# Adds moved from GpSimd to VectorE, probability scaling from VectorE to ScalarE, and later stores, in a two-layer hybrid decoder on one Trainium2 core

## Chip and metric

The kernel runs on one core of one Trainium2 chip. The metric is the device time of one execution in microseconds (us); of several runs the median is taken. Engines are named as the profile names them: PE is TensorE (matrix products), PEld its weight loads, DVE is VectorE, ACT is ScalarE, POOL is GpSimd, and SP is SyncE, which here only issues DMA transfers. Every engine runs its instructions in order.

## What is computed

Two layers over a sequence of 512 positions with model width 2048. Each layer projects x with one wide matrix, runs three groups of attention heads of width 128, gates them, projects back, and normalises. Cut from the reference:

```
h = einsum('bsd,dn->bsn', x, w_in)       # fq fk fv fg | dq dk dv dg | iq ik iw | mq mg
y_fox = fox_attention(fq, fk, fv, cum_logf) * silu(fg)      # 6 heads, causal, forget bias
y_dsa = dsa_attention(rope(dq), rope(dk), dv, index) * silu(dg)   # 6 heads, top 128 keys
kv = einsum('bmd,dn->bmn', mem, w_mem_kv)                   # 256 memory tokens
y_mem = memory_attention(mq, k_mem, v_mem) * silu(mg)       # 4 heads
y = einsum('bsn,nd->bsd', concatenate([y_fox, y_dsa, y_mem]), w_out)
x = layer_norm(ALPHA * x + y, ln_gain, ln_bias)
```

All is float32. In each attention the probabilities are exp(score - max) divided by their row sum.

## The kernel before

**Precision.** A float32 operand is split in two: ACT copies it to a rounded "hi" (`split_hi`), DVE subtracts to get the rest "lo" (`split_lo`). Each product is three matmuls: hi by hi, hi by lo, lo by hi. So each weight half of 128 x 1024 that arrives as tile `raw` becomes `whi` and `wlo` before PE can use it.

**Stages of a layer**, in this order of weight chunks; a chunk has two halves:

- memory: `mv` (4 chunks, memory's values, two halves each) and `mk` (4 chunks, memory's keys). The results are split and stored to DRAM, as `vm` and `km`, and read again when the memory heads run. In layer 1 these chunks also carry, between them, the transposes of the first layer's normalised output (`next_x`).
- small and `iq`: the indexer.
- values (`vs`): twelve blocks of 512 columns of the input projection in six pairs, by a Strassen-like scheme with seven products to a pair: P1, P7, P2, Q6, Q4 (the first part, ten chunks a pair) and Q5, Q3 (the second part). P7's weight is T3, the sum of two blocks of the weight matrix, and Q5's is T1, also a sum. For pair 0 the sum is read from DRAM; for pairs 1 to 5 one block is loaded into `raw` and the other into tiles `other` (two of 512 columns to a half), and `pair_w` adds them, two adds of 128 x 512 for each half. During the first part DVE also selects the indexer's top keys (`top_keys`), one step a chunk, and in layer 1 scales residual rows (`residual_rows`).
- heads: 8 chunks (`c`) of the last query and key projections, between whose products the attention heads run: scores (`s`), Exp, scaling by the reciprocal sums, transposes of the probabilities (`pt`), product with the values (`po`). Rotated heads (d) go through `rope_parts`: two products with cosine and sine tables, then their sum.
- out: the output projection, again seven products to a pair, while the last heads end.

**What sets the order.** The program is written out in Python in one order, and each engine takes its own instructions in that order. Loads are issued by SP two chunks ahead (`load_w(i + 2)`), splits are written three halves ahead (`split_w(n + 3)`), pair adds four (`pair_w(n + 4)`); in each half the pair adds stand ahead of the split. Seven `raw` buffers and four each of `whi` and `wlo` limit how far the loads and the splits really run ahead. Small jobs beside the stream (stores, top keys, residual rows) are generators in a list: `begin(gen, wait)` starts one after `wait` ticks, and `tick` steps all of them; there are two ticks to a chunk, one after the first half and one at its end. Values' accumulating loads (`grow_w`, for Q6 from P7's buffer) are issued by POOL.

The heads are placed by a planner: `Clock` charges each instruction an assumed time on its engine (for ACT 0.00086 us per element and 0.08, plus 0.1 where the scale is a column; for DVE's `tensor_scalar` 0.0007 per element and 0.07), each step of a head names the engine that it needs and the earliest time, and `advance`, called between PE's products, writes the steps that fit. `ahead` adds 0.15 us behind ACT, 0.12 behind DVE and 0.3 behind POOL before the next step may follow. The planned times decide only the order; the real engines wait by semaphores.

**The lines that the change touches.** `pair_w` takes POOL for P7 and DVE for Q5. `rope_parts` adds on POOL. `attend` scales the probabilities with four `nc.vector.tensor_scalar` of 512, 256, 128 and 384 columns, 1280 in all, with the column `rec` as factor; its inner `turn` lets PE's transposes follow at DVE's time. `keep_values` starts the stores of `vm` after 1 tick, and the stores of `km` also start after 1; both are issued by SP.

Of the kernel before, what the change touches and what calls it, by code (L numbers as in the profile page):

```python
# [14 lines left out]
AF = mybir.ActivationFunctionType  # L15
ALU = mybir.AluOpType
# [9 lines left out]
H_FOX, H_DSA, H_MEM = 6, 6, 4  # L26
# [217 lines left out]
def kernel(  # L244
# [13 lines left out]
    clock = Clock()  # L258
    nc = Engines(tc.nc, clock)
# [11 lines left out]
    def uid(name):  # L271
        count[0] += 1
        return f"{name}_{count[0]}"
# [3 lines left out]
    def slot(name, dt=F32, w=512):  # L277
        t = slots.tile([P, w], dt, tag="s", name=uid(name))
        if name in COUNTED:
            out_now.append(t)  # L280
        return t
# [20 lines left out]
    def split_hi(src, hi):  # L302
        nc.scalar.activation(hi, src, AF.Copy)
# [13 lines left out]
    chunks = stream()  # L317
# [16 lines left out]
    def half(src, h):  # L334
        return src[:, h * H:(h + 1) * H]

    def load_w(i, pieces=2, some=(0, 1)):
        if i < len(chunks) and chunks[i][4][0] != "grown":
            kind, key = chunks[i][4]
            src = {"wall": lambda: wall[key], "sum": lambda: sums[key],  # L340
                   "pair": lambda: wall[key[0]]}[kind]()
            if chunks[i][0] == "out" and chunks[i][2][0] == "Q6":
                for h in some:
                    t = [slot("grown") for _ in range(2)]
                    raw.setdefault(i, []).append(t)
                    for c in range(2):
                        nc.sync.dma_start(t[c], half(src, h)[:, c * 512:(c + 1) * 512])
                return
            w = DM // pieces
            for c in range(pieces):  # L350
                if c * 2 // pieces not in some:
                    continue
                if c * 2 % pieces == 0:
                    raw.setdefault(i, []).append(raws.tile([P, H], F32, tag="raw", name=uid("raw")))
                nc.sync.dma_start(raw[i][-1][:, c * w % H:c * w % H + w], src[:, c * w:(c + 1) * w])
                if i < 3 and c * 2 % pieces == 0:
                    load_mem(2 * i + c * 2 // pieces)
                if kind == "pair":
                    for e in (2 * c, 2 * c + 1):
                        t = slot("other")  # L360
                        nc.sync.dma_start(t, wall[key[1]][:, e * 512:(e + 1) * 512])
                        others[i, e] = t

    others = {}

    def pair_w(n):

        i, h = divmod(n, 2)
        if i < len(chunks) and chunks[i][4][0] == "pair":
            for e in range(2):  # L370
                d = raw[i][h][:, e * 512:(e + 1) * 512]
                eng = nc.gpsimd if chunks[i][2][0] == "P7" else nc.vector
                eng.tensor_tensor(d, d, others.pop((i, 2 * h + e)), op=ALU.add)

    def grow_w(n):

# [79 lines left out]
    def load_mem(j):  # L456
        mem_raw[j] = slot("memraw")
        nc.sync.dma_start(mem_raw[j], memt_in[:, j * 512:(j + 1) * 512])
# [122 lines left out]
    km_d = [[dram.tile([P, 512], F32, name=f"km{l}{j}") for j in range(H_MEM)] for l in range(DEPTH)]  # L581
# [6 lines left out]
    def begin(gen, wait=0, last=False, whole=False, but=None):  # L588


        active.append([wait, gen, last, whole, but])
# [20 lines left out]
    ahead = {"PE": 0.2, "ACT": 0.15, "DVE": 0.12, "POOL": 0.3}  # L612
# [25 lines left out]
    def free(n, eng):  # L638
        banks["held"] -= n
        freed.extend([clock.at[eng] + 0.1] * n)  # L640
# [65 lines left out]
    def keep(*moves):  # L706
        for to, t in moves:
            nc.sync.dma_start(to, t.bitcast(F32))
        yield 1

    def keep_values(l, m, part, t):
        c = slice((2 * m + part) * HD, (2 * m + part + 1) * HD)
        begin(keep((vm_d[l].rearrange("h p c -> p h c")[:, :, c],
                    t.rearrange("p (h c) -> p h c", h=H_MEM))), 1)

    def mem_head(l, j):
        there = load_head(("mq", j), MEMQ, j)
# [63 lines left out]
    def rope_parts(ps, to, key):  # L781

        t1, t2 = slot("rope"), slot("rope")
        nc.vector.tensor_tensor(t1, ps, cos_d, op=ALU.mult)
        for a, b, n in HALVES:
            nc.vector.tensor_tensor(t2[a:a + n], ps[b:b + n], sin_d[b:b + n], op=ALU.mult)
        free(1, "DVE")
        yield "POOL",
        nc.gpsimd.tensor_tensor(t1, t1, t2, op=ALU.add)
        yield "ACT",  # L790
        hi, lo = slot("qh", F32R), slot("ql", F32R)
        split_hi(t1, hi)
        yield "DVE",
        split_lo(t1, hi, lo)
        to[key] = (hi, lo)
# [162 lines left out]
    def attend(l, turn_no, kind, h):  # L958
# [17 lines left out]
        else:  # L976
            assert l in chosen
            bt, pr = masks[l], {}
        q, k = qs.pop(key), ks.pop(key)
        del qk_at[key]  # L980
        nm, sums, rec = small("nm", 4), small("sums", 4), small("rec", 4)
# [31 lines left out]
        yield "DVE", 0, 0.0, after(scored, 3)  # L1013
        del q, k
        nc.vector.reciprocal(rec, sums)
        for qb in (3, 1, 0, 2):
            b, off, w = PACK[qb]
            c = slice(off, off + w)
            nc.vector.tensor_scalar(pr[b][:, c], pr[b][:, c], rec[:, qb:qb + 1], None, op0=ALU.mult)
        pt = {}  # L1020

        def turn(tb, kts):
            yield "PE", 1, clock.at["DVE"] + ahead["DVE"]
            tp = bank("pt")
            for kt in kts:
                _, toff = PT_PACK[kt]
                for qb in range(kt, 4):
                    b, off, w = PACK[qb]
                    nc.tensor.transpose(tp[:, toff + (qb - kt) * P:toff + (qb - kt + 1) * P],
                                        pr[b][:, off + kt * P:off + (kt + 1) * P], ident)  # L1030
            yield "ACT",
            w = PT_W[tb]
            both = raws.tile([P, H], F32R, tag="raw", name=uid("pthl")) if w == 512 else slot("pthl", F32R)
            pt[tb] = both[:, :w], both[:, w:2 * w]
            split_hi(tp[:, :w], pt[tb][0])
            yield "DVE",
            split_lo(tp[:, :w], *pt[tb])
            free(1, "DVE")
            turns.append(clock.at["DVE"] + ahead["DVE"])
# [462 lines left out]
    for i, (kind, l, j, col, _) in enumerate(chunks):  # L1502
# [30 lines left out]
        for h in range(2):  # L1533
# [28 lines left out]
            if kind == "out" and late:  # L1562
# [6 lines left out]
                if len(kept) == 16:  # L1569
# [3 lines left out]
                    for c in (0, 256):  # L1573
                        ps = bank("z")
                        c = slice(c, c + 256)
# [19 lines left out]
            elif kind == "mv":  # L1595
                for m in range(2):
                    for nn in range(2):
                        k = 4 * col + 2 * h + nn
                        c = (k % 2) * 256 + m * P
# [3 lines left out]
            elif kind == "mk":  # L1603
                for kk in range(8):
                    k = 8 * h + kk
                    m = memT[k // 2]
                    c = (k % 2) * 256
# [16 lines left out]
        if kind == "mk":  # L1624
            t = slot("kmem", F32R)
            split(ps[:, :256], t[:, 0:256], t[:, 256:512])
            begin(keep((km_d[l][j], t)), 1)
            del t
            if j == 3:
                load_index_tables()  # L1630
        elif kind == "mv" and col == 3:
            for m in range(2):
                hi, lo = slot("vh", F32R), slot("vl", F32R)
                split(out_ps[m], hi, lo)
                for part, t in enumerate((hi, lo)):
                    keep_values(l, m, part, t)
                del hi, lo, t
        elif (kind, j) in HEAD_CHUNKS:
            flow(chunk_parts((kind[0], j), kind[1], ps))
        elif kind == "vs":  # L1640
            if col == 1:
                val_out(name, pair, zs)
                if name in VAL_ENDS:
                    del chains[VAL_CHAIN[name], pair], zs
        elif kind == "small":
            sm = slot("sm")
            nc.scalar.activation(sm, ps, AF.Copy)
            r = slice(96, 96 + H_FOX)
            nc.scalar.activation(sm[r], ps[r], AF.Identity, bias=bfc[r, l:l + 1])
            t = index_rope(ps, 64, 0, nc.vector)  # L1650
            kh2, kl2 = slot("kh2", F32R), slot("kl2", F32R)
            for r in (0, 64):
                nc.scalar.activation(kh2[r:r + 64], t[:64], AF.Copy)
                nc.vector.tensor_tensor(kl2[r:r + 64], t[:64], kh2.bitcast(F32)[:64],
                                        op=ALU.subtract)
            idx["k"] = (kh2, kl2)
            begin(small_work(l, sm))
            del sm, t
        elif kind == "iq":
            t = index_rope(ps, P, P, nc.gpsimd)  # L1660

            begin(index_parts(j, t), 1)
            del t
            if j == 0:
                begin(index_scores(l), 3, last=True, whole=True)
                begin(first_operands(), last=True)
            if j == 7:
                begin(val_operands(), 3, last=True)
            if j == 7:
                index_tabs.clear()  # L1670
# [126 lines left out]
```

## Time and profile before

| | |
|---|---|
| median of 3 runs | 1906.19 us (1903.26 to 1906.65) |
| profiled execution | 1903.6 us, span 1901.8 us |
| granted TensorE clock | 0.998 |
| busy in the span | PE 1876.5 us, DVE 1601.2, ACT 1003.7, POOL 555.7 |
| DMA | 491.01 MB, mean 258 GB/s |

The span is from the first to the last instruction of the profiled execution. In rows of groups, "x80 | 118.2, 1538 | 67.8 <-..." means 80 instructions, 118.2 us busy, 1538 ns each on average, and 67.8 us for which the engine was idle just before them, with what ended that. Rows of the timeline begin with the start in us from the span's start and the duration; square brackets hold the idle time before. All instructions carry line L228, a helper, so they are told apart by their tiles: `v` values, `c` chunks of other projections, `z` output, `pt` transposed probabilities, `bt` and `pr` the probabilities of the two kinds of heads. L355 is the issue of weight loads, L361 that of `other`, L708 the stores of `vm` and `km`. Rows of windows give start, end and length, then busy us and instructions of PE, PEld, DVE, ACT and POOL, the granted clock, the DMA engines' share and GB/s.

### The profile page before, as it was taken

What the parts mean: (1) busy time and instruction counts of PE and PEld (TensorE: products, weight loads), DVE (VectorE), ACT (ScalarE), POOL (GpSimd) and SP (SyncE); (2) the same over time, 40 slices, a digit from 0 to 9 for tenths busy, and PEclk for the clock granted to TensorE, in tenths of its full rate; (3) what the DMA queues carried; (4) which work ended last, traced back from release to release, by engine and by line L of the source; (5) the groups of instructions that cost most, each with busy time, mean ns of one, the idle gap of its engine ahead of it and who ended that gap; (6) DMA issues with size and microseconds to landing.
All of it is one profiled execution on the core that took longest, in us unless ns stands there. A gap on an engine that the chain in (4) does not pass through costs nothing. (4 is left out here: it accounts for less than half of the span.)

```text
span 1901.8 us, 27038 instructions
## 1 busy us (share of the span) xinstructions
PE 1876.5 (99%) x9218; PEld 1596.8 (84%) x9218; DVE 1601.2 (84%) x2519; ACT 1003.7 (53%) x1546; POOL 555.7 (29%) x699
## 2 busy tenths in 40 slices
PE   9999999999999999999999999999999999999997
PEld 8998888888888888888889987788888888888886
DVE  6889788988776888988877898999997768889888
ACT  5676444445455555555476754443454555555552
POOL 0131443333113333230041223443231133342401
PEclk9999999999999999999999999999999999999999
DMA  9886988879999788696578869999799997886965
GB/s 348 288 249 165 288 256 260 286 235 292 337 349 292 190 250 209 212 239 232 176 241 288 263 175 278 293 297 308 238 302 344 342 291 201 262 195 207 305 205 140
DMA packets 198007, 491.01 MB, mean 258 GB/s; under 512 B 19296, under 2 KB 72544, under 8 KB 193004
## 3 DMA queue, kind: packets, MB, share of 16 engines
q1 hardware_dynamic: 158028, 324.60, 49.9%
q0 software_dynamic: 39840, 164.68, 35.2%
q8 instruction: 72, 1.18, 0.2%
q14 instruction: 67, 0.55, 0.1%
HBM read 435.70 MB, written 122.71 MB: 294 GB/s over the span
## 5 line engine op out<-in xcount | busy, mean ns | idle before, releaser
L228 DVE TENSOR_TENSOR wlo<-raw,whi 128x1024 fp32r<-128x1024 f32 (+1 forms) x513 | 671.3, 1317 | 185.6 <-ACT whi L228 181.3
L228 ACT ACTIVATE whi<-raw 128x1024 fp32r<-128x1024 f32 (+1 forms) x513 | 538.8, 1056 | 506.3 <-PE v L228 248.7
L228 PE MATMUL v<-wlo,vxh 128*128 128x512 f32 x768 | 300.0, 391 | 3.6 <-DVE wlo L228 3.6
L228 PE MATMUL v<-whi,vxh 128*128 128x512 f32 x768 | 300.6, 391 | 0.0
L228 PE MATMUL v<-whi,vxl 128*128 128x512 f32 x768 | 299.2, 390 | 0.0
L228 PE MATMUL v<-whi,xh 128*128 128x512 f32 x576 | 224.2, 389 | 0.0
L228 PE MATMUL v<-whi,xl 128*128 128x512 f32 x576 | 224.1, 389 | 0.0
L228 PE MATMUL v<-wlo,xh 128*128 128x512 f32 x576 | 224.1, 389 | 0.0
L228 POOL DMA_DIRECT2D v<-vraw x144 | 94.6, 662 | 419.4 <-ACT vraw L228 230.7
L228 PE MATMUL c<-xh,whi 128*128 128x512 f32 (+1 forms) x544 | 203.7, 374 | 0.0
L228 PE MATMUL c<-xh,wlo 128*128 128x512 f32 (+1 forms) x544 | 198.6, 365 | 0.0
L228 PE MATMUL c<-xl,whi 128*128 128x512 f32 (+1 forms) x544 | 198.1, 364 | 0.0
L228 PEld LDWEIGHTS v<-wlo,vxh 128*128 128x128 f32 x768 | 144.2, 188 | 36.4 <-DVE wlo L228 7.3
L228 PEld LDWEIGHTS v<-whi,vxl 128*128 128x128 f32 x768 | 144.2, 188 | 30.1
L228 PE MATMUL z<-wlo,yh 128*128 128x512 f32 (+1 forms) x434 | 167.9, 387 | 1.2 <-DVE wlo L228 1.2
L228 PEld LDWEIGHTS v<-whi,vxh 128*128 128x128 f32 x768 | 144.3, 188 | 29.5
L228 PE MATMUL z<-whi,yh 128*128 128x512 f32 (+1 forms) x434 | 168.3, 388 | 0.0
L228 PE MATMUL z<-whi,yl 128*128 128x512 f32 (+1 forms) x434 | 167.7, 386 | 0.0
L228 POOL TENSOR_TENSOR raw<-raw,other 128x512 f32<-128x512 f32 x80 | 118.2, 1538 | 67.8 <-DMA other<-in_wall_dram 60.8
L228 PEld LDWEIGHTS v<-whi,xl 128*128 128x128 f32 x576 | 108.1, 188 | 22.6
L228 PEld LDWEIGHTS v<-whi,xh 128*128 128x128 f32 x576 | 108.1, 188 | 22.6
L228 PEld LDWEIGHTS v<-wlo,xh 128*128 128x128 f32 x576 | 108.1, 188 | 22.4
(203 smaller groups left out, 3413.3 us busy)
## 6 DMA issues: line engine op xcount, KB each, us to landing
raw<-in_wall_dram SPq DMA_DIRECT2D x370, 512.0 KB, 7.6
other<-in_wall_dram SPq DMA_DIRECT2D x160, 256.0 KB, 9.0
v<-vraw POOLq DMA_DIRECT2D x144, 256.0 KB, 7.1
sum<-in_wall_dram POOLq DMA_DIRECT2D x32, 1024.0 KB, 11.0
raw<-in_wall_dram POOLq DMA_DIRECT2D x56, 512.0 KB, 7.6
raw<-sum SPq DMA_DIRECT2D x48, 512.0 KB, 6.6
vraw<-v SPq DMA_DIRECT2D x96, 256.0 KB, 6.2
grown<-sum SPq DMA_DIRECT2D x32, 256.0 KB, 6.7
```

The source lines that it names most:

```text
L228: return f(*args, **kw)
```

## The change

Four edits, none of which changes the arithmetic's result in kind:

- T3's adds (P7, pairs 1 to 5, 40 a layer) go from POOL to DVE.
- The rotation's sum (12 a layer) goes from POOL to DVE, ahead of the release of the bank, and the step on POOL falls away.
- The four scalings of a head's probabilities go from DVE to ACT, as Copy with the column as scale, after a step of their own on ACT. The transposes follow ACT's planned time and not DVE's, and 0.3 us more behind it.
- The stores of `vm` start after 4 ticks, those of `km` after 3.

```diff
@@ pair_w
-                eng = nc.gpsimd if chunks[i][2][0] == "P7" else nc.vector
-                eng.tensor_tensor(d, d, others.pop((i, 2 * h + e)), op=ALU.add)
+                nc.vector.tensor_tensor(d, d, others.pop((i, 2 * h + e)), op=ALU.add)
@@ keep_values
-                    t.rearrange("p (h c) -> p h c", h=H_MEM))), 1)
+                    t.rearrange("p (h c) -> p h c", h=H_MEM))), 4)
@@ rope_parts
+        nc.vector.tensor_tensor(t1, t1, t2, op=ALU.add)
         free(1, "DVE")
-        yield "POOL",
-        nc.gpsimd.tensor_tensor(t1, t1, t2, op=ALU.add)
         yield "ACT",
@@ attend
         nc.vector.reciprocal(rec, sums)
+        yield "ACT",
         for qb in (3, 1, 0, 2):
             b, off, w = PACK[qb]
             c = slice(off, off + w)
-            nc.vector.tensor_scalar(pr[b][:, c], pr[b][:, c], rec[:, qb:qb + 1], None, op0=ALU.mult)
+            nc.scalar.activation(pr[b][:, c], pr[b][:, c], AF.Copy, scale=rec[:, qb:qb + 1])
@@ attend, turn
-            yield "PE", 1, clock.at["DVE"] + ahead["DVE"]
+            yield "PE", 1, clock.at["ACT"] + ahead["ACT"] + 0.3
@@ kind == "mk"
-            begin(keep((km_d[l][j], t)), 1)
+            begin(keep((km_d[l][j], t)), 3)
```

More of the change, by code (lines that the diff above doesn't have):

```diff
@@ L359, in load_w @@
                     for e in (2 * c, 2 * c + 1):
-                        t = slot("other")
+                        t = others[i, e] = slot("other")
                         nc.sync.dma_start(t, wall[key[1]][:, e * 512:(e + 1) * 512])
-                        others[i, e] = t
     others = {}
```

## Prediction

> **What bounds the kernel now.** I read the page's first two parts, then TensorE's own waits, then the three places where they fall.
>
> ```profile
> span 1901.8 us, 27038 instructions
> ...
> PE 1876.5 (99%) x9218; PEld 1596.8 (84%) x9218; DVE 1601.2 (84%) x2519; ACT 1003.7 (53%) x1546; POOL 555.7 (29%) x699
> ```
>
> TensorE is busy 99% of the span. The change takes no matmul away, so it can only win what TensorE stands still, 1901.8 - 1876.5 = 25.3 us, or add to it. The view of its waits says what ended those stops:
>
> ```profile
> PE v L228 <- DVE wlo L228: 4.3, 9, 1.1
> PE pt L228 <- DVE pr L228: 2.7, 2, 1.4
> PE pt L228 <- DVE bt L228: 2.0, 2, 1.0
> PE c L228 <- ACT whi L228: 1.9, 1, 1.9
> ...
> PE c L228 <- DVE wlo L228: 0.8, 1, 0.8
> ```
>
> Read as: who waited, for whom, us in all, times, longest. The edits bear on these rows: transposes of probabilities (pt, 2.7 + 2.0), memory's key products (c, 1.9 + 0.8), values (v, 4.3). So at most 11.7 us, 0.6%, is at stake.
>
> **Part 1: probabilities on ACT, with a margin (heads).** One of the four pt stops, in time order:
>
> ```profile
> 675.81 2.63 DVE L228 TENSOR_SCALAR bt<-bt,rec 128x512 f32<-128x512 f32 x4
> 676.30 1.47 POOL L228 TENSOR_TENSOR vl<-vraw,vh 128x512 fp32r<-128x512 f32 x1
> 678.17 0.44 PE L228 MATMUL pt<-ident,bt 128*128 128x128 f32 x2 [1.01 <-DVE bt L228]
> ```
>
> The four scalings took 2.63 us while POOL worked on vl. The planner in the code charges them 0.0007 x 1280 + 4 x 0.07 = 1.18 us and puts the transposes 0.12 us behind. So they were put too early. Averages and what replaces them:
>
> ```profile
> L228 DVE TENSOR_SCALAR bt<-bt,rec 128x512 f32<-128x512 f32 (+3 forms) x48 | 22.6, 532 | 0.4
> L228 DVE TENSOR_SCALAR pr<-pr,rec 128x512 f32<-128x512 f32 (+3 forms) x48 | 18.9, 456 | 0.4
> L228 ACT ACTIVATE bt<-bt,nm 128x512 f32<-128x512 f32 (+3 forms) x48 | 26.5, 556 | 14.3 <-DVE nm L228 14.3
> ```
>
> DVE's batch of four is 4 x 0.456 to 4 x 0.532 = 1.8 to 2.1 us. ACT's Exp over the same four shapes, with a column operand as the new Copy has, is the nearest row: 4 x 0.556 = 2.2 us at most. Charged to ACT is 0.00086 x 1280 + 4 x 0.18 = 1.82, and the transposes then stand 0.15 + 0.3 behind: 1.82 + 0.45 = 2.27 us covers 2.2. So the batch is not shorter; it is charged nearly right, and the 4.7 us of stops should go. ACT must have room, and DVE gives up 41.5 us (22.6 + 18.9), POOL the rotation:
>
> ```profile
> 617.50:821.20 203.70, 201.34 (x1111) 173.23 (x1110) 177.59 (x378) 112.54 (x244) 71.58 (x98) 1.00 0.79 223
> L228 POOL TENSOR_TENSOR rope<-rope,rope 128x512 f32<-128x512 f32 x24 | 36.9, 1538 | 68.6 <-DVE rope L228 34.7 <-PE po L228 25.8 <-PE c L228 6.5
> L228 POOL TENSOR_TENSOR vl<-vraw,vh 128x512 fp32r<-128x512 f32 x24 | 32.4, 1348 | 87.7 <-ACT vh L228 87.6
> L228 DVE TENSOR_TENSOR raw<-raw,other 128x512 f32<-128x512 f32 x80 | 52.0, 685 | 6.4 <-DMA other<-in_wall_dram 6.2
> ```
>
> The window is one layer's heads (columns: PE, its loads, DVE, ACT, POOL). ACT gets 48 x 0.556 = 26.7 us more at most, 112.5 to 139 of 203.7. DVE loses half of 41.5 = 20.8.
>
> **Part 2: rotation's sum on VectorE.** 12 sums a layer (24 in the POOL row). By the raw row, the same shape on DVE, each is 0.685: 8.2 us on DVE, against 12 x 1.538 off POOL. DVE's net in the window is 177.6 - 20.8 + 8.2 = 165 of 203.7. A rotated head is ready 1.538 - 0.685 = 0.85 us sooner. TensorE's list has no wait for it, so I count zero; the cover is the other heads in flight, and without it the 0.85 would count in each. What stays late is vl: 24 x 1.348 on POOL still meets DVE's two-input operations, now the 24 sums too. One hit costs up to 1.35 us. Both parts also change the planner's charges, so the heads' order is new on every engine. Bounds on what is left of stops: 0, and as much as before and again as much (9.4) if no margin holds. I take 1.0, near the low end because the ACT row fits the charge: 4.7 - 1.0 = **-3.7 us**.
>
> **Part 3: memory's stores later.** Layer 1's memory stage, SyncE's queue first:
>
> ```profile
> 954.94 0.33 SPq L355 DMA_DIRECT2D raw<-in_wall_dram  x1
> 967.57 0.38 SPq L708 DMA_DIRECT2D vm<-vh  x1
> 972.39 0.38 SPq L708 DMA_DIRECT2D vm<-vl  x1
> ...
> 973.96 0.73 SPq L355 DMA_DIRECT2D raw<-in_wall_dram  x1
> ...
> 977.07 0.50 SPq L355 DMA_DIRECT2D raw<-in_wall_dram  x1
> ```
> ```profile
> 964.64 1.21 DVE L228 TENSOR_TENSOR wlo<-raw,whi 128x1024 fp32r<-128x1024 f32 x1
> ```
> ```profile
> 987.96 1.06 ACT L228 ACTIVATE whi<-raw 128x1024 fp32r<-128x1024 f32 x1 [3.29 <-DMA raw<-in_wall_dram]
> ```
>
> After the load at 954.94 the queue is held by the first vm store until vh exists (967.57) and by the next until 972.39. Weight loads behind come at 973.96 and 977.07; ACT starts on the latter at 987.96, and TensorE stands 1.9 + 0.8 us. With 4 ticks instead of 1 the four stores go behind three more half loads (mk2's second, mk3's two), which need only raw buffers that splits free, as the one at 964.64. The last then moves from 977.07 up by some 10 us, against a lateness of 2.7. Next in the queue: the vm stores hold the load behind them until vl (972.4), and each km store (3 ticks) holds a half load until kmem is there; those loads serve chunks two further on, which covers it; if not, the stop is as now. The stores are read a stage later, and cost nothing; their slots are held no longer than by vl now. Bounds: 0 and -2.7; I take **-2.5 us**, since ACT's row waits for the load alone.
>
> **Part 4: values' T3 added by VectorE.** Windows cut at the first product of pairs 1 to 4 of layer 1, and one of layer 0:
>
> ```profile
> 317.98:372.38 54.40, 54.40 (x241) 45.05 (x240) 49.59 (x62) 24.17 (x26) 20.25 (x23) 1.00 0.87 255
> ```
> ```profile
> 1146.42:1202.95 56.53, 55.05 (x242) 44.90 (x240) 50.23 (x69) 24.01 (x26) 21.11 (x25) 1.00 0.96 284
> 1202.95:1259.41 56.46, 54.99 (x242) 44.90 (x240) 52.33 (x68) 23.92 (x26) 22.52 (x25) 1.00 0.94 284
> 1259.41:1314.39 54.98, 54.70 (x242) 44.98 (x240) 50.28 (x67) 24.00 (x26) 22.71 (x25) 1.00 0.94 291
> 1314.39:1369.78 55.39, 55.01 (x241) 44.89 (x240) 52.56 (x65) 23.93 (x26) 20.17 (x24) 1.00 0.81 263
> ```
> ```profile
> 1149.51 1.22 DVE L228 TENSOR_TENSOR wlo<-raw,whi 128x1024 fp32r<-128x1024 f32 x1
> 1153.00 3.60 DVE L228 TENSOR_TENSOR wlo<-raw,whi 128x1024 fp32r<-128x1024 f32 x1 [2.27 <-ACT whi L228]
> ...
> 1157.38 5.36 DVE L228 TENSOR_TENSOR wlo<-raw,whi 128x1024 fp32r<-128x1024 f32 x2
> ```
> ```profile
> L228 DVE TENSOR_TENSOR wlo<-raw,whi 128x1024 fp32r<-128x1024 f32 x40 | 58.3, 1481 | 9.2 <-ACT whi L228 9.2
> ```
> ```profile
> L228 POOL TENSOR_TENSOR raw<-raw,other 128x512 f32<-128x512 f32 x80 | 118.2, 1538 | 67.8 <-DMA other<-in_wall_dram 60.8 <-DVE wlo L228 6.7
> ```
>
> ```profile
> PE v L228 <- DVE wlo L228: 3.6, 6, 1.1
> ```
>
> The last row is TensorE's waits in layer 1's values alone: 3.6 of the 4.3. A pair takes 54.40 us where TensorE never waits (layer 0). In layer 1 the first two take 2.1 us more. The cause stands in DVE's rows: a split of 1.22 us becomes 3.60 while POOL adds. The group row covers both pairs: 40 x (1.481 - 1.22) = 10.4, so 5.2 us a pair are lost to this. Eight adds on DVE cost 8 x 0.685 = 5.5 a pair. DVE's sum thus stays: 50.2 + 5.5 - 5.2 = 50.5 of 54.4.
>
> By the Trainium skill, "SBUF — State Buffer", section "Who interferes with whom", a VectorE instruction with two SBUF inputs and a GpSimd one that reads SBUF exclude each other for a whole instruction. The 3.60 agrees. By the rule alone all of v's stops would go, as POOL keeps only DMA issues here: -3.6 in place of the -2.0 taken below, 1.6 less in the sum. It speaks against part 2, whose sums now have two SBUF inputs on DVE.
>
> What it adds is a wait in a queue with other work behind. DVE runs in order: the two adds of a half stand ahead of the split of the half before it. If the T3 block has not landed, DVE stops, with that split, top-key steps, and the release of raw buffers behind. POOL's rows tell how late blocks land:
>
> ```profile
> 1275.05 1.66 POOL L228 TENSOR_TENSOR raw<-raw,other 128x512 f32<-128x512 f32 x1 [0.58 <-DMA other<-in_wall_dram]
> ```
>
> That is the last block of the third pair, 15.6 us after its start. A half is 54.4 / 20 = 2.72 us; the split behind that add is of half 6, counted from 0, needed by its second product at 6 x 2.72 + 2.72 / 12 = 16.55. From landing it takes 0.685 + 1.22 = 1.9, so TensorE stands when a block lands later than 14.6. Here that is 1.0 us.
>
> In layer 0 the loads are early:
>
> ```profile
> 363.11 0.33 SPq L355 DMA_DIRECT2D raw<-in_wall_dram  x1
> ```
> ```profile
> 1261.88 0.50 SPq L355 DMA_DIRECT2D raw<-in_wall_dram  x1
> ```
>
> The same load is issued at 363.1 for the pair that starts at 372.4, 9.3 us ahead, and at 1261.9 for the one that starts at 1259.4, 2.5 behind. So nothing there. Bounds on what is left in values: 0, and 5.5 (the longest stop now, 1.1, in each of five pairs). I take 1.6, the 1.0 of pair 3 and 0.6 allowed in pair 4, nearer the low end since in pairs 1 and 2 it is the lock that stops TensorE: 1.6 - 3.6 = **-2.0 us**. On POOL's queue the accumulating loads that stood behind its adds are issued sooner; no wait of TensorE names them, so zero.
>
> **Sum.** The profiled execution took 1903.6 us, 1.8 around its span. 1903.6 - 3.7 - 2.5 - 2.0 = 1895.4. The median of the three runs, 1906.19, lies 2.6 above that execution; the same gap gives 1898.0. I take 1896.5, between them: 9.7 under the median, 0.5%.
>
> **Rivals.**
> (a) T3's landing takes the place of POOL's lock: values win nothing and lose 2.0 more, up to the 5.5 above: 1896.5 + 2.0 + 2.0 = 1900.5. For: the DMA engines' share of 0.96 in pair 1, a block at 15.6. Against: 67.8 us of idle before POOL's adds is mostly POOL being early.
> (b) The new order of the heads, or vl against the sums, makes new stops as large as the old: 1896.5 + 3.7 = 1900.2. By the Trainium skill, "ScalarE: Activation LUTs", section "Rules for kernel authors", a multiply belongs on VectorE. Rows make it 2.2 against 1.8 to 2.1 us: at worst 0.4 later in each of 24 heads, 9.6 if all were on the path, 1896.5 + 9.6 = 1906.1. The margin of 0.3 and the charge speak against; 3 in 100.
> (c) Memory's later stores do not do what they say, because raw buffers and not the stores hold the loads: 1896.5 + 2.5 = 1899.0.
> (d) Slower: DVE stops at the landing in every pair of both layers. To be 3.8 above 1906.19, this one place must cost 3.8 + 9.7 (all that the forecast wins) + 1.6 = 15.1 us, 1.5 in each of ten pairs; it decides from where last blocks land 14.6 + 1.5 = 16.1 after the pair's start everywhere. Price then 1910 and up. For: layer 1's 15.6. Against: layer 0's loads, 12 us earlier.
>
> **Numbers.** Forecast 0.56, (a) 0.13, (b) 0.16 with the multiply case's 0.03, (c) 0.06, (d) 0.09. About 0.2% (3.8 us) is what a measurement of this kernel can tell from no change: faster is below 1902.4. Faster are the forecast and (a), (b), (c) without the multiply case, 0.56 + 0.32, less 0.11 for two of them together: 0.77. Same is that 0.11, the 0.03, and 0.01 of (d): 0.15. Slower 0.08. The range runs from 1891 (nearly all of the 11.7 against the profiled run) to 1904 (two rivals together); the forecast's own is 1893 to 1900.
>
> **What would show it.** No pt rows above 1 us in TensorE's waits. The c rows gone, and raw loads on SyncE between 955 and 967 in layer 1. Splits of 1.22 throughout values, DVE idle on "other" by a few us, pairs of layer 1 at 54.4 to 55.5. Wrong would be: pt waiting for ACT, v waiting for wlo with "other" before it in DVE's chain, or the out stage waiting for heads.

## The result and the profile after

The changed kernel takes 1894.3 us (median of 4 runs, 1893.35 to 1897.19) against 1906.29 for the kernel before (4 runs, 1903.26 to 1906.65): a ratio of 0.9943, 95% interval 0.9926 to 0.9960. Forecast were 1896.5 us, faster. The two profiled executions differ by 10.5 us in span, 1901.8 to 1891.3; that is less than the 12.0 between the medians, because the profiled execution of the kernel before lies 2.7 us under its median and that of the kernel after 1.0. All differences between traces below are in spans, with one trace to a kernel. In one series the executions of the kernel before took 1903.2 to 1909.9 us, so a difference of 1 or 2 us between two traces alone shows little.

The page's head of the kernel after, and the view of TensorE's waits:

```profile
span 1891.3 us, 27031 instructions
...
PE 1873.4 (99%) x9218; PEld 1597.3 (84%) x9218; DVE 1577.2 (83%) x2527; ACT 1045.7 (55%) x1642; POOL 405.3 (21%) x595
```
```profile
PE v L228 <- DVE wlo L228: 1.8, 3, 1.4
PE warm L228 <- POOL mhalf L228: 1.3, 1, 1.3
PE z L228 <- DVE wlo L228: 1.2, 2, 0.6
PE po L228 <- DVE pthl L228: 0.8, 2, 0.4
PE v L228 <- ACT whi L228: 0.7, 2, 0.4
PE c L228 <- DVE wlo L228: 0.6, 1, 0.6
```

The pt rows (4.7 us before) are gone, c fell from 2.7 to 0.6, v from 4.3 to 1.8. POOL is busy 150 us less.

To see where the time went, the span is cut at the first product of each stage. Each entry is the difference of two start times in the timeline, in us. "idx+val" is the indices and values of a layer, "heads" and "out" the attention's heads and its output product, "mem1" the memory stage of layer 1.

```
                start idx+val0 heads0  out0   mem1 idx+val1 heads1  out1
before          53.70  563.81  161.80 161.65 54.98  569.39  161.89 174.61
after           53.60  563.32  159.57 161.85 52.69  565.80  159.52 174.91
T3 on POOL      53.91  563.55  159.57 161.85 53.17  572.64  159.52 174.54
stores at 1     53.87  563.31  159.57 161.85 54.36  565.88  159.53 174.57
no margin       53.66  563.31  157.77 165.79 54.46  567.28  157.70 178.46
margin 0.15     53.28  563.33  157.76 165.79 53.52  565.48  157.74 178.51
margin 0.6      53.77  563.30  156.00 173.69 52.71  564.80  155.97 185.72
scaling on DVE  53.63  563.31  161.42 163.74 52.89  565.67  161.41 176.63
rotation, POOL  53.23  563.30  155.40 169.01 52.91  568.22  155.36 184.58
POOL's copy     53.86  580.95  159.57 161.84 52.91  591.78  159.53 174.61
adds behind     54.04  563.59  159.62 161.85 52.99  575.39  159.61 174.65
one more slot   53.14  563.32  159.64 161.88 52.71  563.30  159.66 175.04
T3 alone        53.59  563.29  161.86 161.66 56.43  564.53  161.85 174.38
stores alone    53.53  564.58  162.27 161.65 53.47  572.12  161.86 174.61
```

The first two rows say where the 10.5 us came from: heads with out -2.0 and -2.1 in the two layers, memory -2.3, layer 1's indices and values -3.6, and -0.6 in layer 0 ahead of the heads.

Five other rows hold more than their stops. In their traces TensorE's granted clock is 0.50 for a few us (the last 15 us of the span left aside): 6.8 us in each out stage with the margin of 0.6; 3.4 us five times in POOL's copy, twice in adds behind, and once each in no margin (layer 1's indices) and in T3 alone (memory). By an estimate from these figures, up to half of such a stretch is lost.

Layer 1's pairs 1 and 3 in the windows (columns: PE, its loads, DVE, ACT, POOL; then clock, DMA share, GB/s), and DVE's groups over pairs 1 and 2:

```profile
1141.81:1196.20 54.39, 54.39 (x241) 45.05 (x240) 50.15 (x77) 23.82 (x26) 10.97 (x17) 1.00 0.98 299
...
1250.61:1306.66 56.05, 54.69 (x242) 44.97 (x240) 51.70 (x76) 23.91 (x26) 10.36 (x16) 1.00 0.94 284
```
```profile
L228 DVE TENSOR_TENSOR wlo<-raw,whi 128x1024 fp32r<-128x1024 f32 x40 | 47.9, 1220 | 3.9 <-ACT whi L228 3.9
L228 DVE TENSOR_TENSOR raw<-raw,other 128x512 f32<-128x512 f32 x16 | 10.5, 689 | 3.0 <-DMA other<-in_wall_dram 3.0
```

The 40 splits average 1220 ns (before 1481), and pair 1, at a DMA share of 0.98, takes the undisturbed 54.4 us (before 56.53). Only pair 3 is longer. Its place in DVE's timeline, and TensorE's product behind it:

```profile
1264.21 0.69 DVE L228 TENSOR_TENSOR raw<-raw,other 128x512 f32<-128x512 f32 x1 [1.65 <-DMA other<-in_wall_dram]
1266.79 0.69 DVE L228 TENSOR_TENSOR raw<-raw,other 128x512 f32<-128x512 f32 x1 [1.89 <-DMA other<-in_wall_dram]
1267.40 1.22 DVE L228 TENSOR_TENSOR wlo<-raw,whi 128x1024 fp32r<-128x1024 f32 x1
```
```profile
1268.67 0.50 PE L228 MATMUL v<-wlo,vxh 128*128 128x512 f32 x1 [1.36 <-DVE wlo L228]
```

DVE stands 1.89 us for the last T3 block, with a ready split behind the add. TensorE stands 1.36 for that split.

### The profile page after: what moved, and what is told of

The parts are those of the page before. It is cut to its first block, busy times and chain, and to the rows that moved or that the text cites. A ratio compares the mean times of both kernels' runs of the same rounds, so it can differ in the third digit from the quotient of the medians.

```text
span 1891.3 us, 27031 instructions
## 1 busy us (share of the span) xinstructions
PE 1873.4 (99%) x9218; PEld 1597.3 (84%) x9218; DVE 1577.2 (83%) x2527; ACT 1045.7 (55%) x1642; POOL 405.3 (21%) x595
## 4 chain that ended last, share of the span: by engine, by line
PE 84%; issue 6%; DVE 4%; DMA 3%; POOL 1%; ACT 1%; SPq 1%; DVEq 0%; POOLq 0%; ACTq 0%
PE v L228 41%; PE c L228 18%; PE z L228 14%; PE po L228 3%; PE s L228 2%; PE ix L228 2%; DVE wlo L228 1%; DMA other<-in_wall_dram 1%; PE pt L228 1%; DVE z L228 1%; PE qk L228 1%; DMA raw<-in_wall_dram 1%; DMA v<-vraw 1%; DMA z<-x 1%; PE gt L228 1%
## 5 line engine op out<-in xcount | busy, mean ns | idle before, releaser
L228 DVE TENSOR_TENSOR wlo<-raw,whi 128x1024 fp32r<-128x1024 f32 (+1 forms) x513 | 628.5, 1231 | 169.6 <-ACT whi L228 165.8
L228 DVE TENSOR_TENSOR raw<-raw,other 128x512 f32<-128x512 f32 x160 | 103.9, 687 | 15.1 <-DMA other<-in_wall_dram 15.1
```

Source lines behind the costliest of these rows:

```text
L228: return f(*args, **kw)
```

## The experiments

Each ratio is to the kernel before, with its 95% interval; edits are against the kernel after unless said otherwise.

**T3's adds back on POOL.**

```
-                nc.vector.tensor_tensor(d, d, others.pop(...), op=ALU.add)
+                eng = nc.gpsimd if chunks[i][2][0] == "P7" else nc.vector
+                eng.tensor_tensor(d, d, others.pop(...), op=ALU.add)
```

> The changed kernel with T3's adds back on POOL. Lock theory (POOL's two-input adds hold up DVE's splits): pairs 1 and 2 of layer 1 are again about 56.5 us instead of 54.4, TensorE waits for wlo in layer 1's values some 3.6 us instead of 1.4, splits there average 1.4 us or more; time +2 us against the changed kernel (ratio to before about 0.9955). Rival (values gained because the loads or the memory stage ahead of them became earlier, not from where the adds run): pairs stay at 54.4, ratio stays 0.994.

Measured: 1901.05 us, 0.9975 [0.9965, 0.9985]; span +7.5. TensorE's waits:

```profile
PE v L228 <- DVE wlo L228: 5.4, 10, 1.2
```

Ten short stops in place of three; layer 1's indices and values take 6.8 us more, nothing else moves by over half a us. Pairs 1 and 2 take 55.95 and 56.43 us again, and the splits between 1140 and 1310 us average 1398 ns. What the adds meet on POOL is the cause in kind, at more than its expected size.

**T3 on VectorE alone** (the kernel before, with only `nc.vector` in that place).

> The kernel before with T3's adds on DVE and nothing else changed. Theory (the parts add up): layer 1's stage of index and values shrinks by 3.6 us as between the two kernels, to about 566, with one stop left in pair 3; transposes' 4.7 and key products' 2.7 of waits stay; time -3.6 us, ratio 0.998. Rival (with T3 on POOL that stage also gives back what earlier stages win, so that T3 alone is worth what its undoing cost, 6.8 in the stage): the stage at 563, time -6 us, ratio 0.997.

Measured: 1900.1 us, 0.9973 [0.9961, 0.9984]; span -4.2. All of it and a little more lies in layer 1's indices and values, 569.39 to 564.53. The pt rows (2.7 and 2.0) and c (1.8 and 0.8) stay, v falls to 0.8:

```profile
PE pt L228 <- DVE pr L228: 2.7, 2, 1.4
PE pt L228 <- DVE bt L228: 2.0, 2, 1.0
PE c L228 <- ACT whi L228: 1.8, 1, 1.8
...
PE v L228 <- DVE wlo L228: 0.8, 3, 0.4
```

So of the two parts that were tried alone, T3 and the stores, T3 is the larger: 4.9 us in its own stage. Memory's 56.43 holds one of the stretches at half the clock.

**An idle add on POOL beside each of DVE's.** It writes a tile that nothing reads.

```
+                o = others.pop((i, 2 * h + e))
+                nc.vector.tensor_tensor(d, d, o, op=ALU.add)
+                if chunks[i][2][0] == "P7":
+                    nc.gpsimd.tensor_tensor(slot("pad"), o, o, op=ALU.add)
```

> The changed kernel with T3 added on DVE as it is, and besides a POOL add of the same size for each of the 80 (it sums the loaded tile with itself into a scratch tile that nobody reads, so nothing waits for its result). Lock theory: splits that meet it take up to 3.6 us again, average in layer 1's first pairs 1.4 or more, pairs of 55 us and more return, time +2 to +5 us. Rival (the gain came from the adds being shorter on DVE, 0.685 for 1.54, in the chain from landing to split): pairs stay at 54.4, time unchanged.

Measured: 1936.62 us, 1.0150 [1.0134, 1.0165]. TensorE's waits, and DVE's groups between 1140 and 1310 us:

```profile
PE v L228 <- DVE wlo L228: 30.7, 23, 3.6
```
```profile
L228 DVE TENSOR_TENSOR wlo<-raw,whi 128x1024 fp32r<-128x1024 f32 x56 | 69.8, 1265 | 5.8 <-ACT whi L228 5.8
L228 DVE TENSOR_TENSOR raw<-raw,other 128x512 f32<-128x512 f32 x24 | 33.4, 1422 | 3.8 <-DMA other<-in_wall_dram 3.8
```

DVE's add takes 1422 ns in place of 689; nobody waits for POOL's result. The timelines tell the adds apart: 42 of DVE's 160 overlap one of POOL's in time and last 2.03 us on average, the other 118 last 0.68. The difference, 1.35 us, is about one add on POOL (1.32). So POOL's add holds VectorE's up by running at the same time; no data passes from it. The scratch tiles also take slots, and SyncE waits 11.3 us for them between 1140 and 1310 us; but there VectorE waits only 3.8 us for landings, against 6.8 in the kernel after, so the slots are not what held it. The delay fell mostly on the adds, not on the splits as expected, and the price is 44 us of span in place of the 2 to 5 expected: TensorE's waits for wlo make 30.7, and the five stretches at half the clock up to 8.5 (an estimate). The Trainium skill, "SBUF — State Buffer", section "Who interferes with whom", gives this exclusion; here an add of 0.69 us lasted 0.73 longer on average.

**The adds behind the split.** `pair_w(n + 4)` is called after `split_w(n + 3)`, so that a late block no longer holds a ready split.

> The changed kernel with each half's adds written behind the split of the half before, not ahead of it. Theory (in pair 3 of layer 1 DVE stood at a block not yet landed with a split behind): the stop of 1.4 us there goes or shrinks to 0.5 or less, the other pairs stay at 54.4; time -1 us. Rival (DVE is late there by its load of work, not by the landing): the stop stays at 1 us or more.

Measured: 1901.3 us, 0.9966 [0.9954, 0.9979]; layer 1's indices and values +9.6. DVE's waits in pairs 1 and 2 of layer 1, first after, then this kernel:

```profile
DVE wlo L228 <- ACT whi L228: 3.9, 5, 1.3
```
```profile
DVE wlo L228 <- ACT whi L228: 11.0, 10, 2.9
```

The theory fell. The adds of the next half fill the time in which ACT makes the hi part for the split. Put behind it, DVE stands for ACT: 11.0 us in place of 3.9, more than the landing ever cost. Of the 9.6 us, up to 1.7 (an estimate) are a stretch at half the clock at 1277.8 us.

**One more slot.** The pool of large tiles gets one more buffer, paid for by seven kinds of tiny tiles with one buffer in place of two.

```
-    slots = ctx.enter_context(tc.tile_pool(name="slots", bufs=SLOTS))
+    slots = ctx.enter_context(tc.tile_pool(name="slots", bufs=SLOTS + 1))
```

> The changed kernel with one more 128x512 slot in the pool (70 for 69), for which two groups of tiny tiles get one buffer instead of two. Slot theory (in pair 3 of layer 1 the last load of T3 stood 5.0 us in SyncE's queue for a slot that a store of values still held, and so landed 16.2 us after the pair's start): it is issued sooner, lands before 14.6, and the stop of 1.4 us goes or falls to 0.5; time -1 us. Rival (the DMA engines' load, share 0.94 to 0.98 there, sets the landing whatever the issue): landing and stop stay within 0.5 us of what they are.

Measured: 1891.65 us (4 runs, 1890.8 to 1892.66), 0.9921 [0.9908, 0.9934]; span 1888.7. SyncE's waits at the start of pair 3 in the kernel after:

```profile
SPq L361 <- DMA v<-vraw: 5.0, 1, 5.0
SPq L361 <- DMA x<-z: 2.1, 1, 2.1
```

The issue of a T3 block stood 5.0 us until a store of values had landed and left its slot; only then did it go out, at 1259.6. The same pair with one more slot:

```profile
1249.95:1304.35 54.40, 54.40 (x241) 45.05 (x240) 51.60 (x76) 24.30 (x26) 10.40 (x16) 1.00 0.94 289
```

This version is the fastest of all, 2.6 us of span under the kernel after, though the intervals of the two ratios overlap. Layer 1's indices and values take 563.30 us, as layer 0's do (563.32). The pair takes 54.40 at the same DMA share of 0.94: the late landing came from the wait for a slot, not from the transfers' load. DVE has no wait for "other" left between 1250 and 1268.

**Memory's stores at 1 tick again.** `4)` and `3)` back to `1)`.

> The changed kernel with memory's stores after 1 tick again. Theory (stores hold the queue of weight loads): waits of memory's key products go from 0.6 back to about 2.7 us, time +2 us (ratio about 0.9955), loads behind the vm stores issued 10 us later again. Rival (raw buffers hold the loads, the gain came from elsewhere): waits stay at 0.6, ratio 0.994.

Measured: 1895.86 us, 0.9948 [0.9935, 0.9962]. By the intervals this isn't told from the kernel after. In the trace the memory stage takes 1.7 us more, and the stops are back:

```profile
PE c L228 <- ACT whi L228: 1.3, 1, 1.3
PE c L228 <- DVE wlo L228: 0.8, 1, 0.8
```

**The stores alone** (the kernel before, with 4 and 3 ticks).

> The kernel before with only memory's stores later. Theory (the parts are independent): key products' waits 2.7 to about 0.6, the others as before (4.7 of transposes, 3.6 of values), time -2 us, ratio 0.999. Rival (the parts help each other: earlier stages shift loads for the values): values' waits change by 1 us or more too.

Measured: 1904.78 us, 0.9990 [0.9981, 0.9998]. That is the ratio expected. In the trace the memory stage wins 1.5 us, though a stop of 1.5 for a hi part is left at its end, and the values behind it, with T3 still on POOL, take 2.7 more (569.39 to 572.12). That the one causes the other is not shown: the trace of the kernel before is among its fastest executions, and by the medians this version is the faster of the two.

**Scaling on VectorE, with the margin kept behind it.**

```
-        yield "ACT",
-            nc.scalar.activation(pr[b][:, c], pr[b][:, c], AF.Copy, scale=rec[:, qb:qb + 1])
+            nc.vector.tensor_scalar(pr[b][:, c], pr[b][:, c], rec[:, qb:qb + 1], None, op0=ALU.mult)
-            yield "PE", 1, clock.at["ACT"] + ahead["ACT"] + 0.3
+            yield "PE", 1, clock.at["DVE"] + ahead["DVE"] + 0.3
```

> The changed kernel with the scaling back on DVE, the margin of 0.3 kept (behind DVE), the rotation's sum on DVE. Theory (vl alone on POOL still holds up the scaling: 2.6 us against a charge of 1.18 + 0.42): transposes wait 1 us or so at one to four places, 1 to 4 us in all, time +1 to +4 us. Rival (the rotation on POOL was the holder, or the margin is enough): no transposes waiting over 0.3 us, time as the changed kernel.

Measured: 1902.13 us, 0.9975 [0.9967, 0.9984]; span +7.4, heads with out +3.7 and +3.6 in the two layers.

```profile
PE z L228 <- DVE yl L228: 2.4, 2, 1.2
PE po L228 <- DVE pthl L228: 2.1, 4, 0.8
...
PE pt L228 <- DVE pr L228: 0.6, 2, 0.4
```

Here VectorE scales as before, yet the transposes' stops fall from 4.7 to 0.6; whether by the margin or by the rotation's sum having left POOL is not told apart. Other stops come, at the head's product with values (po) and at the output product's operand (z for yl). With this margin the version on ACT is the better one by 7.4 us; but the heads' order is another here too, so this does not show that ACT itself is the better place.

**No margin, half of it, twice it.** `+ 0.3` is left out, or is `+ 0.15`, or `+ 0.6`.

> The changed kernel without the 0.3 us ahead of the transposes. Theory (the move to ACT and its nearly right charge do the work; 1.82 + 0.15 is short of 2.2 at most): transposes wait for ACT a few times, 0.1 to 0.3 us each, under 1 us in all; time within 1 us of the changed kernel, apart from what another order of the heads does. Rival (the margin does the work): waits of the transposes of 2 us and more in all, time +2 us or more.

> The changed kernel with a margin of 0.15 us for 0.3. Cover theory (the margin pays because it spans ACT's real end): the heads and out stages together lie between the changed kernel's 321.4 us a layer and the 323.6 without margin; transposes wait less than 0.3 us in all. Rival (the margin acts by giving the heads another order, which may fall well or ill): no such order, more than 323.6 or less than 321 possible, with stops at the product with the values and at the output's operands, not at the transposes.

> The changed kernel with a margin of 0.6 us for 0.3. Cover theory (0.3 is enough already): heads and out together 321 to 322 us a layer, time within 1 us of the changed kernel. Rival (order): 1.5 us or more away from 321.4 in either direction in each layer, from stops at the product with the values or at the output's operands.

Measured: 1901.25 us, 0.9969 [0.9957, 0.9981] without; 1901.36, 0.9967 [0.9955, 0.9978] with 0.15; 1909.86, 1.0021 [1.0012, 1.0029] with 0.6. In none does a transpose wait; the pt rows are absent from all three. The first with its stop, and the last:

```profile
PE po L228 <- DVE pthl L228: 4.3, 4, 1.7
```
```profile
778.10 0.70 PE L228 MATMUL po<-pthl,vh 128*128 128x512 f32 x2 [1.73 <-DVE pthl L228]
```
```profile
PE po L228 <- DVE pthl L228: 10.9, 4, 5.0
```

In all three the heads stage is shorter than after and the out stage longer by more (157.8 and 165.8 without, 156.0 and 173.7 with 0.6, against 159.6 and 161.9). Products of the out stage start before the last heads are done, and then TensorE stops at a head's po. 0 and 0.15 give the same sums in layer 0 to 0.01 us, and TensorE's products there stand in the same order. With 0.6 the clock falls to half within each of the two stops of 5.0 us and stays there for 6.8 us, in layer 0:

```profile
778.31:785.13 6.82, 5.39 (x17) 4.72 (x17) 6.82 (x12) 2.29 (x4) 0.74 (x2) 0.50 0.92 329
```

So the margin doesn't cover ACT's batch; it decides what order the planner writes, and 0.3 gives a good one while its neighbours on both sides don't.

**Rotation's sum back on POOL.**

```
-        nc.vector.tensor_tensor(t1, t1, t2, op=ALU.add)
         free(1, "DVE")
+        yield "POOL",
+        nc.gpsimd.tensor_tensor(t1, t1, t2, op=ALU.add)
```

> The changed kernel with the rotation's sum back on POOL. Theory (the scaling on ACT no longer meets POOL, so where the rotation is added hardly matters): no waits of the transposes, time within 1 us of the changed kernel. Rival (POOL's sums hold up DVE's other two-input work in the heads): new waits in the heads of 2 us or more in all, time +2 us or more.

Measured: 1903.76 us, 0.9979 [0.9970, 0.9987]; span +10.7. Heads with out +3.0 in layer 0 and +5.5 in layer 1, indices and values of layer 1 +2.4.

```profile
PE v L228 <- DVE wlo L228: 3.9, 6, 2.2
PE z L228 <- DVE yl L228: 2.9, 2, 2.1
...
PE po L228 <- DVE pthl L228: 1.5, 2, 0.7
```

The theory of no effect fell. The stages shift as with the margin (heads shorter, out longer), and the stops at po and yl sum to 4.4 us.

## Why the prediction was right, and where it was off

The parts of the sum make 8.2 us, 2.3 less than the 10.5 between the traces: values were 1.6 short, heads 0.4, memory 0.2 too much, and the 0.6 ahead of layer 0's heads belong to no part.

**Heads, -3.7 forecast, -4.1 measured** (-2.03 and -2.07). The stops to go were named and went. ACT's scalings last 552 ns on average, under the 556 taken from Exp:

```profile
L228 ACT ACTIVATE pr<-pr,rec 128x512 f32<-128x512 f32 (+3 forms) x48 | 23.0, 552 | 2.3 <-DVE rec L228 2.3
L228 ACT ACTIVATE bt<-bt,rec 128x512 f32<-128x512 f32 (+3 forms) x48 | 22.8, 552 | 9.6 <-DVE rec L228 9.6
```

The reason given for it, "1.82 + 0.45 = 2.27 us covers 2.2", is not shown. Without the margin 1.82 + 0.15 = 1.97 covers less than 2.2, and still no transpose waits. What is shown is only that with scaling on ACT these stops are gone at every margin tried, and that with scaling on DVE most of them go too once the margin and the rotation's sum on DVE are there. What is left moved to po: 0.8 us in the view of waits, near the 1.0 allowed. That the term came out so near is in part luck: with the same reasoning and a margin of 0, 0.15 or 0.6, heads and out win at most 0.2 us against the kernel before.

**Rotation, forecast zero.** Here a step failed. "TensorE's list has no wait for it, so I count zero" took each part's price from the stops of the old order. The other sentence of that step, that the charges change and "the heads' order is new on every engine", was the one that counted: back on POOL the sum costs 10.7 us between the traces, and by the ratios (0.9979 against 0.9943) about two thirds of what the whole change wins. The heads' parts have no prices of their own. Undone singly, T3, stores, scaling and rotation cost 7.5 + 1.6 + 7.4 + 10.7 = 27.2 us between single traces, against 10.5 for all together.

**Memory's stores, -2.5 forecast, -2.3 measured.** The size was right; the path was only half seen. SyncE's timeline after, and its waits between 935 and 995 us:

```profile
956.27 0.33 SPq L355 DMA_DIRECT2D raw<-in_wall_dram  x1
972.71 0.33 SPq L1358 DMA_DIRECT2D row<-in_gain_dram  x1
973.15 1.24 SPq L1358 DMA_DIRECT2D row<-in_bias_dram  x1
974.43 0.94 SPq L355 DMA_DIRECT2D raw<-in_wall_dram  x2
975.42 0.94 SPq L707 DMA_DIRECT2D vm<-vh  x1
```
```profile
SPq L355 <- DVE wlo L228: 18.4, 5, 7.8
SPq L1358 <- DVE xl L228: 16.1, 1, 16.1
```

The first load that stood behind the vm stores, issued at 973.96 before, now goes out at 956.27, in the stretch from 955 to 967 that was named. The next one, for which ACT waited 3.29 us and TensorE stopped (977.07 before), did not move by ten us. Behind the load at 956.27 a gain row is next in the queue, and it waits 16.1 us, for what VectorE's work on xl releases. The prediction asked what was next, and named the stores' own waits, not this one. So this load, the first in the x2 row, goes out at 974.43; counted from the stage's first product that is 36.1 us, as before. What changed is its landing: the four stores are behind it in the queue and no longer ahead of it, and it lands 6.5 us after its issue in place of 10.9. Its hi part starts without a wait for it:

```profile
982.76 1.04 ACT L228 ACTIVATE whi<-raw 128x1024 fp32r<-128x1024 f32 x1
```

In all eleven traces with the later stores this load lands 41.0 to 44.2 us after the stage's first product, in the three with 1 tick 46.4 to 47.0. The stage takes 52.7 to 54.5 us in the eleven, and 54.4, 55.0 and 56.4 in the three. That the transfers of the stores were what made it land late fits this, but was not tested apart.

**Values, -2.0 forecast, -3.6 measured between the traces,** and 4.9 when T3 is moved alone. The term that was mis-sized is this one. The mechanism was right: splits at 1220, pairs 1 and 2 at 54.4, and the one stop where it was foretold. In pair 3 the last block landed 16.2 us after the pair's start; the formula, landing less 14.6, gives 1.6, measured are 1.36 in the waits and 1.65 in the pair's length (56.05 - 54.40). What is left was sized right by chance: pair 3 lost 1.65 for the 1.0 foreseen, and the 0.6 allowed for pair 4 did not come. What made the term too small is the 3.6 us that it starts from. That view of waits counts less than the pairs lose: before, pairs 1 to 4 exceed 54.40 by 2.13, 2.06, 0.58 and 0.99, together 5.8. A stop's neighbours cost something too (1.65 against 1.36 in the one stop left). The sum should have been taken from the windows. Of that 5.8, pair 3's 1.65 is what remains, a gain of 4.1 in these pairs; the stage as a whole won 3.6.

"Block lands late" was taken as given. It is a wait of 5.0 us in SyncE's queue for a slot, and one more slot removes it.

**The rivals.** (a), landing in the lock's place, is what happens in pair 3 and nowhere else. (b), an order with new stops, isn't this kernel, but it is every neighbour that was tried in the heads: five of the variants above lose 4 to 15 us in heads and out together (3.9 without margin, 15.5 with 0.6). The chance of 0.16 was too low for a kernel whose order is written by charges. By the multiply rule of the Trainium skill ("ScalarE: Activation LUTs", "Rules for kernel authors") scaling on VectorE would be better. For the single instruction the traces agree, 456 and 532 ns on VectorE against 552 on ScalarE; but the version with scaling on VectorE, in its own order of the heads, is 7.4 us longer, so the instruction's time did not decide. (c) is answered by the load at 956.27 and by the c rows, which came back with 1 tick. (d) needed late blocks everywhere; layer 0's indices and values got no longer (563.81 to 563.32).

**What stays open.** Why just 0.3 gives the good order was not traced through the planner. Whether scaling on ACT or the order that it brings makes the difference to VectorE is not told apart. The values stage with T3 on POOL is longer in two traces whose earlier stages are shorter (572.64 and 572.12 against 569.39); whether that is more than the spread of executions is not known. The 0.6 us ahead of layer 0's heads have no part of the change that was tested for them.

## What to carry to other kernels

Where two engines exclude each other, moving the smaller operation onto the busier engine can be free: eight adds of 0.69 us a pair cost DVE no more than the splits got back, and the time was won. Where a planner orders the work, a moved operation changes the whole order: vary a charge or a margin to both sides before a gain is put down to the thing it was meant for. When a load is late, look first at what the issuing queue waits for (a slot, another store) before transfers are blamed, and take the price of stops from stage lengths, not from the list of waits alone.

## What the hardware showed unexpectedly

An add on POOL without a consumer made the whole kernel 1.5% slower: DVE's adds lasted 2.03 us where they met it and 0.68 where they did not. A stop can cost more than its own length: within the two stops of 5.0 us with the margin of 0.6, TensorE's granted clock fell to 0.50 and stayed there for 6.8 us each time, while the stop of 1.36 us in the kernel after brought no such stretch. And though DMA's share was 0.94 to 0.98 in layer 1's pairs, the transfers did not bound them: pair 3 went from 56.05 to 54.40 us at the same share once its issue wasn't held.
